# Splitting the operands of two LayerNorm sums into two float32r parts

## The chip, the cores and the metric

The kernel runs on one core of one Trainium2 chip. The metric is the device time of one launch in microseconds (us), as the median of several runs. The profile is of one execution; its times are given from the start of its span.

## The reference

The reference is one decoder layer on 1024 tokens of 1024 channels. An input projection feeds two branches: stick-breaking attention with 8 heads, and a convolution branch. Both are gated, merged, projected once more, and normalised with the residual. The change lies in the convolution branch:

```python
c = glu_a * jax.nn.sigmoid(glu_b)
c = causal_depthwise_conv(c, conv_w, conv_b)                    # 512 channels, 31 taps
c = jax.nn.silu(layer_norm(c, conv_ln_g, conv_ln_b))            # over the 512 channels
conv_branch = jnp.einsum('bsc,cd->bsd', c * jax.nn.silu(z_conv), w_conv_proj) + b_conv_proj
```

`layer_norm` subtracts the mean over the channels, divides by the root of the variance plus 1e-5, and applies a gain and an offset.

## The kernel before

Everything stands with channels on the 128 partitions and the 1024 tokens along the free dimension, so the convolution's 512 channels are four tiles `cacc[0]` to `cacc[3]` of 128x1024. Almost every matmul works on float32 data that was split into two float32r parts, a high part (`wh`, `xh`, `tah`, ...) rounded by a copy, and a low part (`wl`, `xl`, `tal`, ...) that is the difference. `mm_piece` (L204 to 217) multiplies one piece of weights, 128x512, into one PSUM bank with three products: high by high, high by low and low by high, twelve matmuls of 512 columns in all.

The instruction order of every engine is fixed when the program is built. A planner, the class `Timeline`, keeps a clock for TensorE (`tl.t`) and for the other engines, with a cost for each operation, and writes an instruction into its engine's queue when its turn comes in that model. Side tasks are generators: one yields an operation for ScalarE ("A"), VectorE ("V") or GpSimd ("G") and goes on when the planner thinks it done. Among operations that are ready for one engine, the planner takes the lowest urgency number first (0 for what frees a PSUM bank, 1 and 2 for most others), and among equals the one that became ready first. On the chip each engine then works through its queue in that order.

`conv_norm` (L610) is the LayerNorm over channels. It adds the four `cacc` tiles on VectorE into `lnsum`. `total` (L617) multiplies the 1024 columns of `lnsum` by a 128x128 matrix of 1/512 (`ones`), as two float32 matmuls of 512 columns, which puts the mean of every token on all partitions of the banks `mps`. Eight subtractions (urgency 0) take the mean from `cacc`. Squares, their sum `lnq` and `variances` follow; a small chain on 128x8 values gives the reciprocal root. Eight instructions spread it onto diagonals (`lndg`, 128x1024), and a second `total` turns it into rows `rps` that all partitions hold. `finish(i)` (L670) multiplies `cacc[i]` by `rps`, takes a sigmoid on ScalarE, applies gain and offset, and multiplies by the sigmoid; two tiles are in work at a time. Before each `total`, `yield tl.now + LAG` holds the matmuls back by 3 us of the planner's clock, so that TensorE, which runs in order, does not stand waiting for them.

This runs beside the stage `run_pairs` (L1022). There pairs of weight blocks, numbered 0 to 11, are multiplied in a scheme with five products per pair here, P5, P6, P7, P4, P3, each one piece of `mm_piece` into a bank `sps`. The pairs follow one another, but the last two are interleaved: P5 and P6 of pair 10, P5 and P6 of pair 11, and then the rest (L863). `make_s(n)` (L899) loads the two blocks of a pair (`rc`, 512 KB each) and forms its operands on VectorE. One buffer `s` serves three of them in turn, so that each step waits until the split of the one before is done: S1 for P5 (`s<-rc`), S2 for P6 (`s<-s,rc`), S4 for P3 (`s<-rc,s`).

```python
        while "S1" not in done:
            yield tl.now + 100
        yield vtt(1, s, s, ra[:, lo_], ALU.subtract)
        have["S2"] = s
```

`split_operand` (L929) makes `wh` on ScalarE and `wl` on VectorE (urgency 1) for each piece. `feed` (L268) lets at most five pieces be split and not yet used up (`N_SPL`). At most two pairs are in work (`N_PAIR`): the loads of pair 11 are issued when the planner sees all five splits of pair 9 done, and S1 of pair 11 is queued when the planner sees the loads landed. Results of the pairs leave PSUM by VectorE (`u`, `c`, urgency 0) in `pair_out`. `split_att` (`attb`, `ach`, `acl`) prepares the attention branch for the matmuls that follow the pairs (`dps<-ach`); it is begun for one of its four tiles at P5 of pairs 8, 9, 10 and 11. The products of the convolution branch start only after the pairs and after `make_cc`, which needs `finish` of all four tiles.

VectorE and ScalarE operations that are issued through helpers show in the profile under the helper's line: L406 (`act`), L409 (`vtt`), L412 (`vstt`). So they are told apart by tile names.

Of the kernel before, what the change touches and what calls it, by code (L numbers as in the profile page):

```python
# [10 lines left out]
F32R = mybir.dt.float32r  # L11
AF = mybir.ActivationFunctionType
ALU = mybir.AluOpType

P = 128
S = 1024
# [7 lines left out]
HALF = 512  # L24
# [150 lines left out]
def layer_kernel(ctx: ExitStack, tc, xT, x, wv, wd, wa, wc, wo, vec, bv, lng, lnb, cst, out):  # L175
    nc = tc.nc
# [7 lines left out]
    tl = Timeline()  # L184
    live = {"ps": 0, "hf": 0}

    def blk(name, dt=F32):
        return blkp.tile([P, S], dt, name=name, tag="blk")
# [5 lines left out]
    def bank(name):  # L194
        live["ps"] += 1
        return psp.tile([P, HALF], F32, name=name, tag="ps")

    def drop(kind, n=1):
        live[kind] -= n

    def f32(ap):
        return ap.bitcast(F32)

    def pe_ns(n):  # L204
        return n / 2.4 + 13.3
# [25 lines left out]
    ones = const.tile([P, P], F32, name="ones")  # L231
    nc.vector.memset(ones, 1.0 / (NC * P))
    ones_r = const.tile([P, P], F32R, name="ones_r")
# [4 lines left out]
    def vcol(i, rows=slice(0, P)):  # L238
        return vecs[rows, i:i + 1]
# [165 lines left out]
    def act(u, out, in_, func=AF.Copy, n=HALF, **kw):  # L405
        return "A", u, n, (lambda: nc.scalar.activation(out, in_, func, **kw)), (BIAS if "bias" in kw else {})  # L406

    def vtt(u, out, a, b, op, n=HALF):
        return "V", u, n, lambda: nc.vector.tensor_tensor(out, a, b, op=op)  # L409

    def vstt(u, out, a, s, b, op0, op1, n=HALF, ptr=True):
        return "V", u, n, (lambda: nc.vector.scalar_tensor_tensor(out, a, s, b, op0, op1)), (PTR if ptr else {})  # L412
# [126 lines left out]
    def start_cc():  # L539
        if flags["conv"] and flags["pairs"]:  # L540
            for i in range(NC):
                tl.spawn(make_cc(i), tl.now)
# [28 lines left out]
    def conv_block(i):  # L571
# [21 lines left out]
        def last():  # L593
            yield vtt(9, b[:, ev], b[:, ev], a[:, ev], ALU.subtract)
            yield vtt(9, a[:, 1:HALF], a[:, 1:HALF], a[:, HALF:S - 1], ALU.add, HALF)
            yield vtt(9, a[:, od], b[:, ev], a[:, od], ALU.subtract)
            yield "V", 9, S, lambda: nc.vector.tensor_scalar(a, a, vcol(CONVB + i), None, op0=ALU.add), {"per": 0.521}
            conv_stat["on"] -= 1
            conv_stat["done"] += 1
            start_conv()  # L600
            if conv_stat["done"] == NC:
                tl.spawn(conv_norm(), tl.t)
# [7 lines left out]
    def conv_norm():  # L610
        hs = [slice(0, HALF), slice(HALF, S)]
        s = blk("lnsum")
        yield vtt(1, s, cacc[0], cacc[1], ALU.add, S)
        for i in (2, 3):
            yield vtt(1, s, s, cacc[i], ALU.add, S)

        def total(src, name):  # L617
            r = [bank(name) for _ in hs]
            for ps, c in zip(r, hs):
                nc.tensor.matmul(ps, ones, src[:, c], start=True, stop=True)  # L620
                tl.t += 4 * pe_ns(HALF)
            return r

        got = []
        yield tl.now + LAG
        yield lambda: got.extend(total(s, "mps"))
        mps = list(got)
        yield [vtt(0, cacc[i][:, c], cacc[i][:, c], ps, ALU.subtract) for i in range(NC) for ps, c in zip(mps, hs)]
        drop("ps", 2)
        q = None  # L630
        for i in range(NC):
            qi = blk(f"lnq{i}")
            yield act(0, qi, cacc[i], AF.Square, n=S)
            if i:
                yield vtt(1, q, q, qi, ALU.add, S)
            else:
                q = qi


        def variances():  # L640
            ps = bank("vps")
            for b in range(NT):
                nc.tensor.matmul(ps[:, b:b + 1], q[:, b * P:(b + 1) * P], ones[:, 0:1], start=b == 0, stop=b == NT - 1)
                tl.t += 4 * 109
            return ps

        got.clear()
        yield tl.now + LAG
        yield lambda: got.append(variances())
        vps = got[0]  # L650
        lt = blk("lnt")
        sd, r, t2 = (lt[:, k * NT:(k + 1) * NT] for k in range(3))
        yield "A", 0, NT, lambda: nc.scalar.activation(sd, vps[:, 0:NT], AF.Sqrt, bias=epsc[:, 0:1]), {"extra": 1300}
        yield "V", 1, NT, lambda: nc.vector.reciprocal(r, sd), {"per": 6.2}
        yield vtt(1, t2, r, r, ALU.mult, NT)
        yield vstt(1, t2, vps[:, 0:NT], epsc[:, 0:1], t2, ALU.add, ALU.mult, NT)
        drop("ps")
        yield "V", 1, NT, lambda: nc.vector.tensor_scalar(t2, t2, -0.5, 1.5, op0=ALU.mult, op1=ALU.add), {"per": 0.521}

        yield vstt(1, r, r, float(NC * P), t2, ALU.mult, ALU.mult, NT, ptr=False)  # L660
        dg = blk("lndg")
        yield [("V", 1, P, (lambda b=b: nc.vector.tensor_scalar(dg[:, b * P:(b + 1) * P], ident, r[:, b:b + 1], None,
                                                               op0=ALU.mult)), {"per": 0.521}) for b in range(NT)]
        got.clear()
        yield tl.now + LAG
        yield lambda: got.extend(total(dg, "rps"))
        rps = list(got)
        left, left_r = [NC], [NC]

        def finish(i):  # L670
            a, g = cacc[i], blk(f"lng{i}")
            yield [vtt(1, a[:, c], a[:, c], ps, ALU.mult) for ps, c in zip(rps, hs)]
            left_r[0] -= 1
            if left_r[0] == 0:
                drop("ps", 2)
            yield act(0, g, a, AF.Sigmoid, n=S, bias=vcol(LNB + i), scale=vcol(LNG + i))
            yield "V", 1, S, lambda: nc.vector.tensor_scalar(a, a, vcol(LNG + i), vcol(LNB + i), op0=ALU.mult,
                                                             op1=ALU.add), {"per": 0.521}
            yield vtt(1, a, a, g, ALU.mult, S)
            left[0] -= 1  # L680
            if left[0] == 0:
                flags["conv"] = True
                start_cc()
            elif i + 2 < NC:
                tl.spawn(finish(i + 2), tl.now)

        for i in range(2):
            tl.spawn(finish(i), tl.now)
# [420 lines left out]
    for k in range(NK):  # L1109
# [9 lines left out]
        for c0 in range(0, S, step):  # L1119
            c = slice(c0, c0 + step)  # L1120
# [133 lines left out]
    def cuts(tb):  # L1254
        return [0, HALF, HALF + 256, D] if tb == NT - 1 else [0, HALF, D]
# [43 lines left out]
    for d in range(NK):  # L1299
        while not {2 * d, 2 * d + 1} <= wo_there:  # L1300
            tl.skip()
        for tb in range(first):
            for n in range(2):
                tt, c = slice(tb * P, (tb + 1) * P), slice(n * HALF, (n + 1) * HALF)
# [9 lines left out]
    for tb in range(first, NT):  # L1314
        load_row(tb)
        tt = slice(tb * P, (tb + 1) * P)
        for n in range(len(cuts(tb)) - 1):
            c = slice(cuts(tb)[n], cuts(tb)[n + 1])
# [3 lines left out]
            ps = bank("yps")[:, 0:w]  # L1322
# [30 lines left out]
    c = slice(0, N_TAIL)  # L1353
# [56 lines left out]
```

## Time and the profile before

| | |
|---|---|
| median of 3 runs | 760.25 us (759.88 to 760.5) |
| profiled execution, its own time | 760.05 us |
| its span | 758.2 us |
| mean granted TensorE clock | 0.997 |
| TensorE busy (matmul) | 743.2 us, 98% |
| VectorE busy | 624.1 us, 82% |
| ScalarE busy | 348.4 us, 46% |

The time is the span plus 1.85 us around it. Busy shares are means over stages with different limits. In the lists an instruction is shown by engine, line, operation and `out<-in` tiles; a matmul's duration is longer than the step from one to the next, since they are pipelined.

### The profile page before, as it was taken

To read this page: it belongs to the slowest core of one execution; us is meant where nothing else is said; L and a number is where in the kernel's file an instruction comes from. 1 tells how busy PE (TensorE), PEld (TensorE's weight loads), DVE (VectorE), ACT (ScalarE), POOL (GpSimd) and SP (SyncE) were. 2 spreads that over 40 slices of the span, in tenths; PEclk is the share of its full clock that TensorE was granted. 3 is DMA by queue.
4 is the path that set the end of the run, shared out by engine and by line. 5 is a ranking of instruction groups with operands and counts; after the bars stand their busy time and mean duration, and the time that the engine had idled before them with its cause. 6 is when DMAs were issued, how large, how long until landed. Compare 5 with 4: busy or idle time off the path is not lost.

```text
span 758.2 us, 10189 instructions
## 1 busy us (share of the span) xinstructions
PE 743.2 (98%) x3630; PEld 622.8 (82%) x3630; DVE 624.1 (82%) x950; ACT 348.4 (46%) x652; POOL 117.5 (15%) x128
## 2 busy tenths in 40 slices
PE   9999999999999999999999999999999999999995
PEld 7888888889888888888888888787878888888885
DVE  7537779999998639999999999999996759920985
ACT  2119757279677745876443433355542323410100
POOL 3312330413432332040200000000000033000000
PEclk9999999999999999999999999999999999999998
DMA  7553543544754448286653453355547865530052
GB/s 229 181 189 114 98 91 63 98 97 78 170 110 103 85 71 192 56 246 207 176 200 131 155 178 123 132 190 168 207 153 239 282 228 198 198 117 1 0 202 75
DMA packets 51972, 110.60 MB, mean 146 GB/s; under 512 B 6225, under 2 KB 11217, under 8 KB 51922
## 3 DMA queue, kind: packets, MB, share of 16 engines
q1 hardware_dynamic: 41474, 96.26, 37.5%
q0 software_dynamic: 10304, 13.64, 12.4%
q8 instruction: 28, 0.46, 0.2%
q14 instruction: 22, 0.18, 0.1%
q10 hardware_dynamic: 144, 0.07, 0.0%
HBM read 81.62 MB, written 24.12 MB: 139 GB/s over the span
## 4 chain that ended last, share of the span: by engine, by line
PE 79%; DVE 17%; issue 1%; ACT 1%; DMA 1%; POOL 0%; SPq 0%; DVEq 0%; ACTq 0%; POOLq 0%
PE dps L216 11%; PE dps L211 10%; PE dps L212 10%; PE sps L211 7%; PE sps L212 7%; PE sps L216 7%; PE vps L1130 6%; DVE cacc L412 5%; PE pvps L777 4%; PE yps L222 4%; PE yps L223 4%; PE yps L224 4%; PE tps L754 4%; DVE f L739 3%; DVE cs L412 2%; PE zps L727 1%
## 5 line engine op out<-in xcount | busy, mean ns | idle before, releaser
L211 PE MATMUL dps<-xh,wh 128*128 128x512 f32 x352 | 141.1, 401 | 0.0
L212 PE MATMUL dps<-xl,wh 128*128 128x512 f32 x352 | 137.6, 391 | 0.0
L216 PE MATMUL dps<-xh,wl 128*128 128x512 f32 x352 | 99.3, 396 | 0.0
L739 DVE TENSOR_TENSOR_SCAN f<-f,eyez 128x896 f32<-128x896 f32 (+3 forms) x64 | 83.2, 1341 | 5.8 <-ACT f L406 5.8
L412 DVE SCALAR_TENSOR_TENSOR cacc<-cin,vecs,cacc 128x511 f32<-128x511 f32 (+14 forms) x116 | 82.7, 739 | 0.0
L252 POOL TENSOR_TENSOR wl<-wr,wh 128x512 fp32r<-128x512 f32 x22 | 30.9, 1410 | 302.5 <-ACT wh L248 302.5
L212 PEld LDWEIGHTS dps<-xl,wh 128*128 128x128 f32 x352 | 66.3, 188 | 12.3
L211 PEld LDWEIGHTS dps<-xh,wh 128*128 128x128 f32 x352 | 66.2, 188 | 12.3
L216 PEld LDWEIGHTS dps<-xh,wl 128*128 128x128 f32 x352 | 64.0, 188 | 11.9
L248 ACT ACTIVATE wh<-wr 128x512 fp32r<-128x512 f32 x80 | 50.5, 636 | 46.6 <-DMA wr<-wv 26.6
L796 POOL DMA_DIRECT2D att<-pvt x64 | 56.5, 991 | 95.1 <-ACT pvt L406 61.3
L406 ACT ACTIVATE wth<-tps 128x384 fp32r<-128x384 f32 (+1 forms) x80 | 43.7, 567 | 45.0 <-PE tps L754 44.4
L409 DVE TENSOR_TENSOR wtl<-tps,wth 128x384 fp32r<-128x384 f32 (+1 forms) x80 | 48.9, 628 | 18.7 <-ACT wth L406 17.7
L255 POOL DMA_DIRECT2D wl<-wd x36 | 32.9, 915 | 125.2 <-ACT wl L254 89.5
L223 PE MATMUL yps<-wol,mh 128*128 128x512 f32 (+1 forms) x136 | 51.2, 377 | 0.0
L224 PE MATMUL yps<-woh,ml 128*128 128x512 f32 (+1 forms) x136 | 51.2, 376 | 0.0
L222 PE MATMUL yps<-woh,mh 128*128 128x512 f32 (+1 forms) x136 | 51.2, 376 | 0.0
L754 PE MATMUL tps<-eyez,f 128*128 128x128 f32 x288 | 42.9, 275 | 2.6 <-DVE f L739 2.6
L412 DVE SCALAR_TENSOR_TENSOR cs<-cs,hs__77 128x511 f32<-128x511 f32 (+14 forms) x60 | 44.3, 739 | 0.1
L412 DVE SCALAR_TENSOR_TENSOR xrow<-xrow,yps 128x512 f32<-128x512 f32 (+1 forms) x17 | 10.7, 653 | 39.8 <-PE yps L224 39.7
L406 ACT ACTIVATE f<-zps 128x384 f32<-128x384 f32 (+2 forms) x96 | 40.2, 530 | 3.3 <-PE zps L727 3.2
L777 PE MATMUL pvps<-wtl,v 128*128 128x256 f32 (+1 forms) x160 | 40.2, 287 | 0.7 <-DVE wtl L409 0.3
(173 smaller groups left out, 1689.1 us busy)
## 6 DMA issues: line engine op xcount, KB each, us to landing
wr<-wd SPq DMA_DIRECT2D x56, 256.0 KB, 3.0
rc<-wd SPq DMA_DIRECT2D x24, 512.0 KB, 5.7
wl<-wd POOLq DMA_DIRECT2D x36, 256.0 KB, 4.9
c<-c SPq DMA_DIRECT2D x36, 256.0 KB, 2.4
att<-pvt POOLq DMA_DIRECT2D x64, 64.0 KB, 3.4
ga<-c SPq DMA_DIRECT2D x8, 512.0 KB, 6.5
wor<-wo SPq DMA_DIRECT2D x16, 256.0 KB, 6.2
gc<-c SPq DMA_DIRECT2D x8, 512.0 KB, 6.8
```

Source lines behind the costliest of these rows:

```text
L211: nc.tensor.matmul(ps, wh[:, kk], mh, start=first and kk is ks[0], stop=False)
L212: nc.tensor.matmul(ps, wh[:, kk], ml, start=False, stop=False)
L216: nc.tensor.matmul(ps, wl[:, kk], mh, start=False, stop=last and kk is ks[3])
L222: nc.tensor.matmul(ps, wh, mh, start=first, stop=False)
L223: nc.tensor.matmul(ps, wh, ml, start=False, stop=False)
L224: nc.tensor.matmul(ps, wl, mh, start=False, stop=last)
L406: return "A", u, n, (lambda: nc.scalar.activation(out, in_, func, **kw)), (BIAS if "bias" in kw else {})
L412: return "V", u, n, (lambda: nc.vector.scalar_tensor_tensor(out, a, s, b, op0, op1)), (PTR if ptr else {})
L739: u.ready[tb] = yield ("V", 2, n, lambda: nc.vector.tensor_tensor_scan(f[:, 0:n][:, ::-1], f[:, 0:n][:, ::-1], eyez[:, S - n:S][:, ::-1], ...
L754: nc.tensor.transpose(ps[:, o:o + P], u.f[tb][:, j * P:(j + 1) * P], ident)
L777: nc.tensor.matmul(u.ps[:, 0:n], st, wt[:, jj * 256:jj * 256 + n], start=(i == m and jj == 0 and wt is wh), stop=(i == 0 and jj == 1 and w ...
L796: e = yield "G", 1, 0, (lambda part=part: nc.gpsimd.dma_start(dst, tmp[part, 0:256], accum_op=ALU.add)), {"extra": 430}
```

## The change

Before each of the two sums, a new generator `parted` makes two float32r tiles of the 128x1024 operand: a copy on ScalarE (high part) and a subtraction on VectorE (low part). `total` then multiplies each 512-column half of both parts by `ones_r`, a float32r copy of the same matrix that the kernel already holds, and adds them in PSUM. The planner's charge for one half falls from four matmul steps to two. Two more blocks are taken from the pool of 128x1024 tiles for each sum. `variances` keeps float32.

```diff
             for ps, c in zip(r, hs):
-                nc.tensor.matmul(ps, ones, src[:, c], start=True, stop=True)
-                tl.t += 4 * pe_ns(HALF)
+                for part in src:
+                    nc.tensor.matmul(ps, ones_r, part[:, c], start=part is src[0], stop=part is src[1])
+                tl.t += 2 * pe_ns(HALF)
             return r
 
+        def parted(src, name, got):
+
+            h, l = blk(f"{name}h", F32R), blk(f"{name}l", F32R)
+            yield act(1, h, src, n=S)
+            yield vtt(1, l, src, f32(h), ALU.subtract, S)
+            got.extend((h, l))
+
         got = []
+        sp = []
+        yield from parted(s, "lnsum", sp)
         yield tl.now + LAG
-        yield lambda: got.extend(total(s, "mps"))
+        yield lambda: got.extend(total(sp, "mps"))
...
         got.clear()
+        dp = []
+        yield from parted(dg, "lndg", dp)
         yield tl.now + LAG
-        yield lambda: got.extend(total(dg, "rps"))
+        yield lambda: got.extend(total(dp, "rps"))
```

## Rows read from the trace of the kernel before

**Rows 1.** Page, part 1: busy us (share of the span) and instructions of two engines.

```profile
PE 743.2 (98%) x3630; PEld 622.8 (82%) x3630; DVE 624.1 (82%) x950; ACT 348.4 (46%) x652; POOL 117.5 (15%) x128
```

**Rows 2.** Busy time by stretch, us: length, PE, PEld, DVE, ACT, POOL, granted clock, DMA share.

```profile
474.00:486.00 12.00, 12.00 (x51) 9.24 (x50) 11.93 (x18) 3.52 (x7) 0.00 (x0) 1.00 0.45 155
486.00:502.00 16.00, 16.00 (x72) 13.26 (x71) 15.96 (x25) 9.02 (x13) 0.00 (x0) 1.00 0.41 132
502.00:520.00 18.00, 18.00 (x85) 14.45 (x84) 16.98 (x38) 9.82 (x14) 0.00 (x0) 1.00 0.48 159
520.00:540.00 20.00, 20.00 (x90) 16.57 (x89) 20.00 (x31) 10.62 (x15) 0.00 (x0) 1.00 0.65 217
540.00:560.00 20.00, 18.12 (x78) 14.09 (x77) 19.20 (x32) 8.94 (x15) 0.00 (x0) 1.00 0.64 232
560.00:577.00 17.00, 17.00 (x76) 14.08 (x76) 16.64 (x28) 8.28 (x14) 0.00 (x0) 1.00 0.31 103
```

**Rows 3.** Waits of PE from 370 to 758 us: total us, times, longest.

```profile
PE sps L211 <- ACT wh L406: 1.9, 2, 1.3
```

**Rows 4.** Timeline of PE, 550 to 557 us: start, duration, [idle before <- releaser].

```profile
552.63 0.50 PE L211 MATMUL sps<-tah,wh 128*128 128x512 f32 x1 [1.28 <-ACT wh L406]
...
556.24 0.50 PE L211 MATMUL sps<-tah,wh 128*128 128x512 f32 x1 [0.60 <-ACT wh L406]
```

**Rows 5.** Timeline of DVE: operand steps and splits of pair 9, S1 of pair 11.

```profile
523.48 0.68 DVE L409 TENSOR_TENSOR wl<-s,wh 128x512 fp32r<-128x512 f32 x1
...
527.61 0.68 DVE L409 TENSOR_TENSOR s<-s,rc 128x512 f32<-128x512 f32 x1
...
537.99 0.69 DVE L409 TENSOR_TENSOR s<-rc,s 128x512 f32<-128x512 f32 x1
...
543.93 0.68 DVE L409 TENSOR_TENSOR wl<-s,wh 128x512 fp32r<-128x512 f32 x1
...
551.14 0.69 DVE L409 TENSOR_TENSOR s<-rc 128x512 f32<-128x512 f32 x1
```

**Rows 6.** Timeline of DVE: where the LayerNorm's steps stand.

```profile
478.77 1.22 DVE L409 TENSOR_TENSOR lnsum<-lnsum,cacc 128x1024 f32<-128x1024 f32 x1
...
485.56 4.87 DVE L409 TENSOR_TENSOR cacc<-cacc,mps 128x512 f32<-128x512 f32 x8
...
517.31 2.47 DVE L409 TENSOR_TENSOR cacc<-cacc,rps 128x512 f32<-128x512 f32 x4
...
539.80 1.22 DVE L409 TENSOR_TENSOR cacc<-cacc,lng 128x1024 f32<-128x1024 f32 x1
```

**Rows 7.** Chain that ended last, 478 to 519 us: start, share of the chain, what.

```profile
480.93 1.72 PE mps L620 x4
...
513.10 0.91 PE sps L216 x4
...
514.46 1.72 PE rps L620 x4
```

**Rows 8.** Groups of instructions: count, busy us, mean ns of one.

```profile
L409 DVE TENSOR_TENSOR tbl<-tb,tbh 128x1024 fp32r<-128x1024 f32 x4 | 4.9, 1218 | 0.0
...
L406 ACT ACTIVATE tah<-ta 128x1024 fp32r<-128x1024 f32 x4 | 4.2, 1056 | 0.0
```

**Rows 9.** Timeline of DVE: a 1024-wide operation and the next one's start.

```profile
534.33 1.22 DVE L409 TENSOR_TENSOR cacc<-cacc,lng 128x1024 f32<-128x1024 f32 x1
535.46 0.69 DVE L409 TENSOR_TENSOR wl<-rc,wh 128x512 fp32r<-128x512 f32 x1
```

**Rows 10.** Timeline of DVE and PE: last split of the attention operands, first and later matmuls on them.

```profile
572.45 0.69 DVE L409 TENSOR_TENSOR acl<-attb,ach 128x512 fp32r<-128x512 f32 x1
575.46 0.39 PE L211 MATMUL dps<-ach,wh 128*128 128x512 f32 x1
...
579.76 0.39 PE L212 MATMUL dps<-acl,wh 128*128 128x512 f32 x1
```

## The prediction

> **What bounds the kernel now.** I read the page's busy shares first, then busy time by stretch around the LayerNorm, then what TensorE waited for, then the timelines of TensorE and VectorE there. TensorE is busy 98% of the span [rows 1], so what shortens its work can show in full, as long as nothing else takes the time back. By stretches [rows 2] the reader is to see two things. TensorE has no gap from 474 to 540 us, and again from 560 on, but it lacks 1.88 us between 540 and 560. And VectorE, whose share over the whole span is only 82%, is here as full as TensorE: 11.93 + 15.96 + 16.98 + 20.00 + 19.20 = 84.07 us of the 86 us from 474 to 560. The LayerNorm runs in just this stage. The waits of TensorE say that from 370 us to the end it stood still only twice, 1.9 us together, both times for a `wh` of ScalarE [rows 3]; its timeline puts them at 552.63 (1.28 us) and 556.24 (0.60 us) [rows 4]. From 474 to 577 us the stage has two bounds close together, TensorE's own work and VectorE's queue.
>
> **Why TensorE stood still there.** Going back from 552.63: that matmul is P5 of pair 11, and its `wh` is a copy of S1 of pair 11, which VectorE made at 551.14 [rows 5]. That step's place in VectorE's queue was given by the planner: the loads of pair 11 come after the last split of pair 9. Followed in the queue, pair 9 goes: split of S1 at 523.48, S2 at 527.61, S4 at 537.99, split of S4 at 543.93, done 544.6 [rows 5]. From there to 551.14 are 6.5 us, which the planner reserves for the loads of 1 MB. So each wait in VectorE's queue on the way from 523 to 544 us pushes P5 of pair 11 out. What filled that queue was `finish`: its first multiplication by `rps` stands at 517.31, its last product at 539.80 [rows 6], over the same 20 us.
>
> **The change, part by part.**
>
> *Matmuls.* In the chain the four instructions of a float32 `total` (two per half) hold TensorE 1.72 us, and four float32r matmuls of 512 columns hold it 0.91 us [rows 7]. After the change a `total` is four float32r matmuls. Each saves 1.72 - 0.91 = 0.81 us, both 1.62 us. That those four run at the pace of the neighbours is what I take; they have the same form, 128x128 weights with 512 float32r columns. The bounds are 0 (they run as slow as float32) and 1.62.
>
> *ScalarE.* Two more copies of 128x1024 at 1.06 us [rows 8], 2.1 us together. ScalarE is busy 3.52 of 12 us from 474 and 9.82 of 18 us from 502 [rows 2], so its idle time covers them. Without that cover the price would be a `wh` later by up to 1.06 us, which the splits made ahead take up.
>
> *VectorE.* Two more subtractions of 128x1024, like `tbl<-tb,tbh` at 1218 ns [rows 8]. They are pipelined: after a 1024-wide one that began at 534.33 the next began at 535.46 [rows 9], so each takes 1.13 us of the queue, 2.26 us together. Nothing hides these by itself: VectorE has 86 - 84.07 = 1.93 us free before 560 [rows 2]. Behind them in the queue stand the splits `wl`, the operands `s`, and the PSUM reads. The bounds of what they cost TensorE are 0, if its stock of splits covers them, and 2.26 us, if all of it arrives at 556.24.
>
> *Order.* The chain of the LayerNorm grows twice by a copy (1.06 us) and a subtraction (1.13 us) ahead of the 3 us of LAG, plus a turn behind one or two 0.6 us operations, less the 0.81 us that `total` takes less: by about 2 us each time. With the first subtraction's own 1.13 us in the queue, `finish` begins some 4 to 5 us later, at about 522 instead of 517.31. This is not a cost by itself: the convolution's products come after the pairs, behind 577 us, and `finish` was over at 541 [rows 6]. But it moves 12 us of VectorE work (8 at 0.60, 4 at 0.72, 4 at 1.13) against the splits of pair 9. At the head of pair 9's chain, before 523, some 4 us of `finish` no longer stand in front of the split of S1 and of S2; these come about 4 us earlier, and the later links (split of S2, S4, split of S4) stay in the crowd as before. Pair 9 is then done at about 541 rather than 544.6, S1 of pair 11 stands at about 547.5 rather than 551.14, and P5 of pair 11 could start at 549. TensorE was ready for it at 552.63 - 1.28 = 551.35 and would be now at 551.35 - 1.62 = 549.7. So the first stop of 1.28 us goes. The second, 0.60 us, lies in the steps S1, split, S2, copy of pair 11 itself; I leave it as it is. The bounds of the stop are 0 and, with all 2.26 us of VectorE and the earlier arrival of TensorE, 1.88 + 1.62 + 2.26 = 5.8 us.
>
> *Blocks.* Four more tiles are taken from the pool of 43. The kernel's tiles alive at this point, counted in the code, are at most about 40, so I cost this at nothing; if one had to wait, it would be a load `rc`, on SP's queue, and pair 11 would be later again.
>
> *Sum.* 760.05 - 1.62 - 1.28 = 757.15 us for the profiled execution; the median shown lies 0.2 us above it, so 757.4 us.
>
> **A rule that speaks against it.** The row shows TensorE stopped behind ScalarE and VectorE, with VectorE full [rows 2, 4]. The Trainium skill, "Perfetto Trace Analysis", section "Optimization Strategies", says that where the matmul engine is idle waiting for others, it is those others that should be relieved. This change loads one of them more. By the rule the sum would be 760.25 + 2.26 = 762.5 us, and the trace bears out its condition, that VectorE has no room; whether its later work or its place in the order decides, the rows of before can't tell. That is the second rival below.
>
> **The rivals.**
>
> *The stop stays, the matmuls save.* The two stops are 1.88 us as before, because the later `finish` falls on the later links of pair 9 and on pair 10 as hard as it fell on the earlier ones. For it: 20.00 of 20 us busy from 520 to 540, wherever one puts things. The time is 760.25 - 1.62 = 758.6 us.
>
> *VectorE's queue sets the end of the stage* (the other side). S1 of pair 11 comes later by up to the 2.26 us that were added, and the matmuls' saving only makes TensorE wait longer at the same place. After 556.24 TensorE has no gap, so the whole time moves by what that matmul moves: 760.25 + 2.26 = 762.5 us. Where half of it is taken up by VectorE's free 1.93 us, it is about 761, within what counts as no change. It decides from the point where pair 9's last split comes later than 543.93. Against it: from 523 to 544 us more than half of the links' time was waiting behind others in the queue, and part of those others leaves.
>
> *The change gives nothing at the matmuls*, since the float32r sums run no faster or the planner moves another task into their place: about 760.25 - 0.3 or so. Against it: the neighbours' 0.91 us [rows 7].
>
> *The attention products become the next stop.* If the pairs end 3.5 us earlier, the first `dps<-ach` come at 572 instead of 575.46. The last `acl` ended at 573.1, and its matmul ran at 579.76 [rows 10]: 6.6 us of room, less 3.5, less 2.26 of later VectorE. That leaves 0.8 us, so nothing is lost; if the order is worse there, some 1 to 2 us.
>
> **How the numbers follow.** A run's median here tells differences of about 0.2%, or 1.5 us. Both stops shrink or the first goes (757.4; with both gone 756.75): 0.42. The stop stays (758.6, just past the bound): 0.18. The stop grows by about what the matmuls save, or they save nothing (759 to 761.7): 0.23. VectorE sets the end (about 762.5): 0.12. Something else, such as a late load or the attention operands, to either side: 0.05. Faster by over 0.2%: 0.42, two thirds to three quarters of 0.18, and a little of the last, 0.57. Slower by over 0.2%: 0.12 and some of the neighbouring cases, 0.16. Within: 0.27. The range goes from 756.5, both stops gone, to 761.7, where a good part of VectorE's 2.26 us comes through; the full 762.5 is left out.
>
> **What would show it.** In the changed kernel's profile: `mps` and `rps` with four matmuls each, 0.91 us in the chain instead of 1.72; two subtractions and two copies of 128x1024 more; the first `cacc<-cacc,rps` near 522; S1 of pair 11 at 549 or earlier; and TensorE's wait for `wh` near 0.6 us. The prediction is wrong if that wait is 3 us or more, if TensorE waits at a new place between 480 and 580 us (for a `wl`, for `acl`, or at the sums themselves for the low part, should VectorE run behind the planner's clock by more than the 3 us of LAG), or if the gap-free stretch after 580 us is broken.

## The result, and the profile after

The changed kernel took 764.64 us (763.93 to 766.72, 4 runs) beside 760.38 us for the kernel before on the same chip; the ratio is 1.0057, 95% interval 1.0045 to 1.0069. So it became slower by about 4.3 us, where 2.9 us less was forecast, and the time lies outside the range. Single runs of one kernel scatter by 1 to 3 us, because the first part of the program, which is the same in all, ends later in some: in the fourteen profiled executions TensorE either began 11 to 13 matmuls from 6 to 9 us, and the first addition of `lnsum` stood at 475.3 to 475.9 us, or it began 7, and the addition stood at 476.8 to 478.3. Where two traces are set side by side below, times are therefore also counted from that addition, which stands at 475.30 us in the profiled execution before and at 477.09 in the one after.

The waits of TensorE from 370 us to the end, which answer to [rows 3]:

```profile
PE sps L216 <- DVE wl L409: 2.6, 2, 2.3
PE sps L211 <- ACT wh L406: 2.1, 1, 2.1
```

They were 1.9 us, all for a `wh`; now they are 4.8 us, and more than half is for a `wl` of VectorE. The timeline of TensorE shows the places, beside [rows 4]; the last rows show its pace:

```profile
550.67 1.19 PE L216 MATMUL sps<-tah,wl 128*128 128x512 f32 x4 [0.37 <-DVE wl L409]
...
555.94 2.01 PE L216 MATMUL sps<-tah,wl 128*128 128x512 f32 x4 [2.26 <-DVE wl L409]
560.10 0.79 PE L211 MATMUL sps<-tah,wh 128*128 128x512 f32 x1 [2.15 <-ACT wh L406]
...
561.12 0.63 PE L211 MATMUL sps<-tah,wh 128*128 128x512 f32 x1
561.54 0.63 PE L212 MATMUL sps<-tal,wh 128*128 128x512 f32 x1
...
568.56 0.39 PE L211 MATMUL sps<-tbh,wh 128*128 128x512 f32 x1
...
569.01 0.39 PE L211 MATMUL sps<-tbh,wh 128*128 128x512 f32 x1
569.24 0.39 PE L212 MATMUL sps<-tbl,wh 128*128 128x512 f32 x1
```

The first of the three waits, 0.37 us, is for the `wl` of P6 of pair 10. P5 of pair 11 now gets its `wh` in time, but stands for its `wl`; P6 of pair 11 stands for its `wh`. And there is a second loss that is no wait: from 556 to 566 us matmuls of 512 columns follow one another every 0.43 us instead of every 0.23. Busy time by stretch names it (length, PE, PEld, DVE, ACT, POOL, granted clock, DMA share):

```profile
550.00:554.00 4.00, 3.31 (x14) 2.17 (x12) 4.00 (x7) 0.00 (x0) 0.00 (x0) 1.00 0.98 365
554.00:558.00 4.00, 2.01 (x4) 1.09 (x4) 4.00 (x7) 0.80 (x2) 0.00 (x0) 0.76 0.60 210
558.00:562.00 4.00, 1.90 (x5) 1.52 (x6) 4.00 (x8) 2.02 (x4) 0.00 (x0) 0.50 0.01 4
562.00:566.00 4.00, 4.00 (x11) 3.12 (x10) 2.78 (x5) 1.82 (x3) 0.00 (x0) 0.50 0.00 0
566.00:570.00 4.00, 4.00 (x19) 3.25 (x18) 3.35 (x7) 0.63 (x1) 0.00 (x0) 0.96 0.00 0
```

The granted clock is 0.50 from 558 to 566, that is 1.2 instead of 2.4 GHz. The trace has its fall at 556.0 us, just behind the stop of 2.26 us, so that the four matmuls from 555.94, 2.01 us long, are already slow; it is back at 1.00 from 566.3, with TensorE at work without a gap since 560.10. In the kernel before it stayed at 1.00 through both its stops [rows 2]. The Trainium skill, "TensorE: Matmul & The Clock Gate", section "Part 1: The HAM clock gate (the "warmup" mystery)", says that the lower clock is the default and activity releases it; the trace agrees, with the fall behind a stop and the rise in a gapless stretch.

VectorE's timeline, from the first product by `rps` to the stops, beside [rows 5] and [rows 6]:

```profile
524.94 1.88 DVE L409 TENSOR_TENSOR cacc<-cacc,rps 128x512 f32<-128x512 f32 x3
...
541.29 0.68 DVE L409 TENSOR_TENSOR cacc<-cacc,rps 128x512 f32<-128x512 f32 x1
...
548.01 0.68 DVE L409 TENSOR_TENSOR s<-rc 128x512 f32<-128x512 f32 x1
...
550.54 1.21 DVE L409 TENSOR_TENSOR cacc<-cacc,lng 128x1024 f32<-128x1024 f32 x1
...
553.48 1.21 DVE L409 TENSOR_TENSOR cacc<-cacc,lng 128x1024 f32<-128x1024 f32 x1
...
555.21 0.68 DVE L409 TENSOR_TENSOR wl<-s,wh 128x512 fp32r<-128x512 f32 x1
...
558.22 0.68 DVE L409 TENSOR_TENSOR s<-s,rc 128x512 f32<-128x512 f32 x1
```

S1 of pair 11 (`s<-rc`) did come early: 70.92 us after the first addition of `lnsum`, where it had been 75.84. Its `wh` was done at 549.5 on ScalarE. But its `wl` stands at 555.21, behind the last steps of `finish` for the third and fourth tile, and S2 (558.22), which needs that split done, after it. In the kernel before, `finish` was over at 541 [rows 6].

The sums themselves did what was said; the chain for the first one, beside [rows 7] (the four matmuls of `rps` follow one another every 0.23 us too):

```profile
485.44 0.91 PE mps L621 x4
```

**Where the 6.67 us between the two profiled executions are** (766.72 and 760.05). The first addition of `lnsum` is 1.79 us later; that is the scatter of the start. From there to P6 of pair 11 it takes 83.01 us instead of 80.94: 2.07 more. That is 1.62 less for the sums, 2.90 more of waiting (0.37 + 2.26 + 2.15 - 1.88), and 0.80 for the four matmuls between the stops at the low clock (1.71 instead of 0.91). From P6 of pair 11 to the second piece after it takes 8.46 us (560.10 to 568.56) instead of 5.62 (556.24 to 561.86): 2.84 for the clock. Together 6.70. Without the start, some 4.9 us belong to the change in these two executions, within the 3.4 to 5.2 of the interval. The line of the kernel before at which that second piece begins:

```profile
561.86 0.39 PE L211 MATMUL sps<-tbh,wh 128*128 128x512 f32 x1
```

### The profile page after: what moved, and what is told of

Its sections match the earlier page's. It is cut to its first block, busy times and chain, and to the rows that moved or that the text cites. A ratio compares the mean times of both kernels' runs of the same rounds, so it can differ in the third digit from the quotient of the medians.

```text
span 765.0 us, 10206 instructions
## 1 busy us (share of the span) xinstructions
PE 746.9 (98%) x3630; PEld 626.7 (82%) x3630; DVE 626.5 (82%) x952; ACT 350.9 (46%) x654; POOL 116.3 (15%) x128
## 4 chain that ended last, share of the span: by engine, by line
PE 77%; DVE 19%; issue 2%; ACT 1%; DMA 1%; POOL 0%; SPq 0%; DVEq 0%; ACTq 0%; POOLq 0%
PE dps L216 11%; PE dps L211 10%; PE dps L212 10%; PE sps L211 6%; PE sps L212 6%; PE sps L216 6%; PE vps L1142 6%; DVE cacc L412 5%; PE pvps L789 4%; PE yps L224 4%; PE yps L223 4%; PE yps L222 4%; PE tps L766 4%; DVE f L751 3%; DVE cs L412 2%
```

## The experiments

All are compared with the kernel before on the same chip. The columns of the table: the ratio with its interval; P6 of pair 11, counted from the first addition of `lnsum`; the stops of TensorE at pairs 10 and 11; VectorE's work and idle time from that addition to S2 of pair 11; and the first `yps` matmul, counted from that addition too, which holds everything the change can do and not the scatter of the start. All but the ratio are from the profiled execution, so they are of one execution each. From the first `yps` to the end every kernel here takes the same 95.7 to 95.8 us.

| kernel | ratio (interval) | P6 of pair 11 | stops | work + idle | first yps |
|---|---|---|---|---|---|
| before | 1 | 80.94 | 1.88 | 78.33 + 1.13 | 187.2 |
| changed | 1.0057 (1.0045 to 1.0069) | 83.01 | 4.78 | 80.06 + 1.07 | 192.1 |
| matmuls alone | 1.0009 (1.0001 to 1.0018) | 81.14 | 3.71 | 78.83 + 0.82 | 187.4 |
| operands alone | 1.0076 (1.0064 to 1.0088) | 85.14 | 4.38 | 80.28 + 3.35 | 191.8 |
| delay alone | 1.0074 (1.0061 to 1.0087) | 83.66 | 4.52 | 78.13 + 3.66 | 191.5 |
| work alone | 1.0073 (1.0061 to 1.0086) | 85.08 | 5.88 | 80.77 + 2.42 | 193.2 |
| low parts on GpSimd | 1.0082 (1.0068 to 1.0096) | 85.23 | 7.50 | 81.36 + 2.39 | 193.9 |
| first sum only | 1.0017 (1.0007 to 1.0027) | 80.96 | 3.16 | 78.44 + 1.01 | 188.8 |
| second sum only | 1.0049 (1.0034 to 1.0063) | 82.96 | 4.64 | 80.54 + 0.89 | 192.0 |
| shorter LAG | 1.0061 (1.0045 to 1.0077) | 83.24 | 5.61 | 80.33 + 1.00 | 190.8 |
| stops filled | 1.0022 (1.0011 to 1.0033) | 83.03 | 1.46 | 80.07 + 1.07 | 189.3 |
| before, finish last | 0.9967 (0.9954 to 0.9979) | 78.41 | 0 | 68.67 + 1.17 | 184.5 |
| changed, finish last | 0.9958 (0.9945 to 0.9970) | 76.68 | 0 | 72.27 + 1.07 | 182.8 |
| changed, late half last | 0.9941 (0.9926 to 0.9956) | 76.69 | 0 | 72.76 + 1.07 | 182.8 |

### The matmuls alone

Against the kernel before, the lines that matter (`lndg` becomes float32r like `lnsumr`, and the planner's charge is that of the change):

```diff
-        for i in (2, 3):
-            yield vtt(1, s, s, cacc[i], ALU.add, S)
+        sr = blk("lnsumr", F32R)
+        yield vtt(1, s, s, cacc[2], ALU.add, S)
+        yield vtt(1, sr, s, cacc[3], ALU.add, S)
...
-                nc.tensor.matmul(ps, ones, src[:, c], start=True, stop=True)
...
+                for n in range(2):
+                    nc.tensor.matmul(ps, ones_r, src[:, c], start=n == 0, stop=n == 1)
...
-        yield lambda: got.extend(total(s, "mps"))
+        yield lambda: got.extend(total(sr, "mps"))
...
-        dg = blk("lndg")
+        dg = blk("lndg", F32R)
```

> The float32r matmuls of the change without its copies and subtractions: lnsum's last addition and the diagonals are written as float32r at once, and each half adds that one part twice (so the low part is left out and the sum is doubled). Theory A (the time went into where finish now falls against the splits of pairs 10 and 11, because the chain grew by a copy and a subtraction): finish stays about where it was or begins up to 1 us earlier, the stops stay near 1.9 us, TensorE's clock stays at full speed in the pairs, and the time is 1 to 2 us below before. Rival (any shift of the order costs 3 us and more): 762 or more.

It came out about level with before, not 1 to 2 us faster. `finish` began where it was, but its last product moved from 64.5 to 68.2 us after the first addition, and the stops grew by 1.83 us, about what the sums saved (1.62). P6 of pair 11 stood where it was, within 0.2 us: TensorE only came to wait earlier. So VectorE's queue sets that point, and cheaper matmuls ahead of it gain nothing. The expectation missed this. The granted clock stayed at 1.00 in this execution, though its first stop was 2.67 us long.

### The operands alone

Against the kernel before; `parted` is that of the change, and `total` keeps its float32 matmuls:

```diff
+        sp = []
+        yield from parted(s, "lnsum", sp)
         yield tl.now + LAG
         yield lambda: got.extend(total(s, "mps"))
...
+        dp = []
+        yield from parted(dg, "lndg", dp)
         yield tl.now + LAG
         yield lambda: got.extend(total(dg, "rps"))
```

> The change's copies and subtractions with the old float32 matmuls (the parts are made and not used). Theory A: finish begins some 6 us later as in the change, TensorE's stops in the pairs are 4 us or more, the clock falls to half speed after them, and the time is 4 to 7 us above before, 1.6 us more than the change at most. Rival B (the float32r matmuls themselves or the planner's shorter charge for them cause it): within 1 us of before or at most 2.3 us above it.

5.8 us above before by the ratio, as the first theory said. Its `finish` moved further than that theory had it: the first product by `rps` comes 10.2 us later than in the kernel before, not some 6. The loss comes with the operands; the float32r matmuls are not its cause.

### The delay alone

```diff
-        yield tl.now + LAG
+        yield tl.now + LAG + 2200
         yield lambda: got.extend(total(s, "mps"))
...
-        yield tl.now + LAG
+        yield tl.now + LAG + 3700
         yield lambda: got.extend(total(dg, "rps"))
```

> The kernel before with the two float32 sums held back by 2.2 and 3.7 us more of the planner's clock, and nothing added to any engine. Theory A (the place of finish decides, not the 2.26 us of VectorE work): the stops grow to 3 us or more and the time is 2 to 6 us above before. Rival C (the added work on VectorE decides): within 1 us of before.

5.6 us slower with no work added to any engine. Busy time by stretch, beside the third of [rows 2]:

```profile
502.00:520.00 18.00, 18.00 (x89) 15.18 (x88) 15.07 (x33) 9.69 (x15) 0.00 (x0) 1.00 0.47 160
```

VectorE, which had 16.98 us of work in these 18 us, has 15.07. The work that it could not yet do lies behind, in front of the splits of pairs 10 and 11: 3.66 us idle ahead of S2 of pair 11 instead of 1.13, and P6 of pair 11 comes 2.72 us later. So added work on VectorE is not needed to be slow, and neither are the copies on ScalarE or the four tiles from the pool, which this kernel does not have.

### The work alone

```diff
+        def extra(src, name):
+            yield vtt(1, blk(name), src, cacc[0], ALU.subtract, S)
...
+        tl.spawn(extra(s, "ex0"), tl.now)
         yield tl.now + LAG
...
+        tl.spawn(extra(dg, "ex1"), tl.now)
         yield tl.now + LAG
```

> The kernel before with two more 128x1024 subtractions on VectorE at the places of the two low parts, that nobody waits for, and no other change. Rival C (the added 2.26 us on VectorE decides): the stops grow by about 2 us and the time is 2 us or more above before. Theory A (the place of finish decides): the price is smaller than that of the delay alone (5 us), 0 to 2.5 us.

5.5 us slower. Nobody waits for these two subtractions, and yet the whole price is there; the expectation that the work alone costs less than the delay alone fell. The reason is in the table: the 2.26 us of work went ahead of S2 of pair 11 in full (2.44 more), and since the LayerNorm's own steps stand behind it in the queue, these moved too (the last product of `finish` to 554.3), with 1.29 us more of idle time. So work and delay are not two theories; here either puts the late half of `finish` on the splits of pairs 10 and 11.

### The low parts on GpSimd

```diff
-            yield vtt(1, l, src, f32(h), ALU.subtract, S)
+            yield "G", 1, S, lambda: nc.gpsimd.tensor_tensor(l, src, f32(h), op=ALU.subtract)
```

> The changed kernel with the two low parts made on GpSimd, which is idle in this stage, instead of VectorE: VectorE has its old amount of work, and the chain grows by more than in the change. Theory A (the place of finish decides): stops of 3 us or more and a time of 2 to 6 us above before. Rival C (VectorE's added work decides): the stops are back at about 1.9 us and the time is 1 to 2 us below before.

6.2 us slower, though VectorE has its old amount of work in all: the later chain put 3.0 us more of it ahead of S2 of pair 11 (81.36 against 78.33). So taking the work off the full engine is not enough while the chain grows.

### One sum of the two

```diff
-        yield from parted(dg, "lndg", dp)
...
-        yield lambda: got.extend(total(dp, "rps"))
+        yield lambda: got.extend(total32(dg, "rps"))
```

`total32` is the old `total`.

> The change for the mean's sum alone; the second sum keeps float32. Counted from the first addition of lnsum, P6 of pair 11 began 80.94 us later in the kernel before and 83.01 in the changed one. Theory Q (VectorE works without a gap and in order, and all of finish stands ahead of pair 11's S2, so that each us of work or of idle time put ahead of it arrives there): 82.0 to 82.5, and the time is 1 to 1.5 us above before, or up to 4 if the stop is long enough for the clock to fall. Theory A (the place of finish alone): finish moves by half as much, the stops are between, 80 to 83, without a rule.

> The change for the second sum (the reciprocal roots) alone; the mean's sum keeps float32. Theory Q: P6 of pair 11 at 82.0 to 82.5 us after the first addition of lnsum, the time 1 to 1.5 us above before, up to 4 with the clock. Theory A: as for e9, between 80 and 83.

The second is the same edit on `lnsum`, with the change left for `lndg`. Each adds 1.13 us of VectorE work. The first left P6 of pair 11 where it was (80.96) and cost 1.3 us by the ratio, with one stop of 3.16 us and a clock of 0.87 from 560 to 570; since P6 of pair 11 did not move and the first `yps` came 1.6 us later, its whole loss lies behind that stop, in the slow matmuls. The second moved it by 2.02 us, nearly as far as both together. So the rule that each microsecond put ahead arrives, which had both at 82.0 to 82.5, does not hold: in the one case the planner put as much other work behind S2 as came in front (78.44 against 78.33), in the other it put 2.2 us ahead for 1.13 added.

### A shorter LAG

```diff
-        yield tl.now + LAG
+        yield tl.now + LAG - 1500
         yield lambda: got.extend(total(sp, "mps"))
...
-        yield tl.now + LAG
+        yield tl.now + LAG - 2500
         yield lambda: got.extend(total(dp, "rps"))
```

> The changed kernel with the waits ahead of the two sums cut by 1.5 and 2.5 us, which brings finish back to within some 2 us of its old place; the added work stays. Theory A (the place of finish): P6 of pair 11 near 81.3 us after the first addition of lnsum, the clock at full speed, and the time within 1 us of before. Theory Q: the work ahead is the same, so P6 of pair 11 stays at 82.5 to 83.2, and the time is 1 to 4.5 us above before.

As slow as the change. It tells less than it was meant to: the first product by `rps` came back by 1.8 us, but the last of `finish` by only 0.4, so the late half stayed on the same splits.

### The stops filled

In `mm_piece`, with `fill[0]` at 1 for P5 of pair 11, at 2 for P6 of pair 11 and at 0 otherwise:

```diff
+        fills = (fill[0] in (1, 2)) * 9
+        if fill[0] == 2:
+            for _ in range(fills):
+                nc.tensor.matmul(ps, zero_r, movs[0][0], start=True, stop=True)
...
+        if fill[0] == 1:
+            for _ in range(fills):
+                nc.tensor.matmul(ps, zero_r, movs[0][0], start=False, stop=False)
         for kk, (mh, ml) in zip(ks, movs):
             nc.tensor.matmul(ps, wl[:, kk], mh, start=False, stop=last and kk is ks[3])
```

> The changed kernel with nine more matmuls of 512 columns on weights of zero in front of the low-part matmuls of P5 of pair 11, and nine in front of P6 of pair 11, into the bank of that piece; they add nothing to the result and the planner doesn't charge them. Theory D (about 3 us of the loss is the clock, which fell to half speed after the stops): the granted clock stays at full speed in the pairs, and the time is 2 to 3.5 us below the change (761 to 762.5). Rival (the slow matmuls after the stops cost nothing, since VectorE sets the pace there): the same time as the change, 764 to 765, or up to 1 us more.

TensorE did eighteen matmuls more and the kernel was faster than the changed one: a ratio of 1.0022 instead of 1.0057, 2.7 us. Its timeline:

```profile
550.69 1.20 PE L225 MATMUL sps<-tah,wl 128*128 128x512 f32 x4 [0.37 <-DVE wl L420]
...
555.97 1.21 PE L225 MATMUL sps<-tah,wl 128*128 128x512 f32 x4 [0.22 <-DVE wl L420]
...
560.13 0.50 PE L217 MATMUL sps<-tah,wh 128*128 128x512 f32 x1 [0.87 <-ACT wh L417]
```

The three ends of waiting are the same as in the changed kernel within 0.03 us, so VectorE sets them. What differs is the clock after them, at 1.00 in stretches that showed 0.50:

```profile
558.00:562.00 4.00, 3.13 (x14) 2.14 (x13) 4.00 (x8) 2.06 (x4) 0.00 (x0) 1.00 0.00 0
562.00:566.00 4.00, 4.00 (x20) 3.31 (x19) 3.90 (x7) 2.31 (x4) 0.00 (x0) 1.00 0.00 0
```

The first `yps` comes 2.8 us earlier than in the changed kernel, the 2.84 us read from the trace above. What is left, 2.1 us over before, is the later end of the stops.

### finish behind the splits

```diff
-            yield [vtt(1, a[:, c], a[:, c], ps, ALU.mult) for ps, c in zip(rps, hs)]
+            yield [vtt(2, a[:, c], a[:, c], ps, ALU.mult) for ps, c in zip(rps, hs)]
...
-            yield "V", 1, S, lambda: nc.vector.tensor_scalar(a, a, vcol(LNG + i), ...)
-            yield vtt(1, a, a, g, ALU.mult, S)
+            yield "V", 2, S, lambda: nc.vector.tensor_scalar(a, a, vcol(LNG + i), ...)
+            yield vtt(2, a, a, g, ALU.mult, S)
```

This was done on the changed kernel, on the kernel before, and on the changed kernel for the third and fourth tile alone (`u = 1 if i < 2 else 2`).

> The changed kernel with the VectorE steps of finish at urgency 2 instead of 1, so that the splits and operands of the pairs go before them. Theory A: the stops at pairs 10 and 11 shrink to under 1 us, the clock stays at full speed, and the time is 1.5 to 3.5 us below before (757 to 759). Rival C (VectorE has too little room for 2.26 us more, whatever the order): 761 or more.

> The kernel before with the VectorE steps of finish at urgency 2, as in e4_after_finish_last. Theory A: with the splits first there is no stop at pairs 10 and 11 or hardly one, so the time is 1 to 1.9 us below before (758.4 to 759.3), and e4, which has the two cheaper sums besides, lies 1.3 to 1.8 us below this one. Rival (the gain of e4 comes all from the order, the float32r sums being worth nothing): as fast as e4, 757.

> The changed kernel with the VectorE steps of finish at urgency 2 for the third and fourth tile alone, those that fell on the splits of pairs 10 and 11. They are 4 at 0.60, 2 at 0.72 and 2 at 1.13 us, 6.1 us, more than the two stops of 4.4 us that can be read at P5 and P6 of pair 11. Theories Q and A: no stop or under 0.5 us, the clock at full speed, the time within 0.7 us of e4_after_finish_last (757.0). Rival (it takes both halves, or the gain of e4 came from elsewhere): 759 or more.

All three were faster than before, at medians of 757.01, 758.72 and 756.96 us. By the ratios the kernel before gained 2.5 us, more than its 1.88 us of stops and than the 1 to 1.9 expected; what the rest is stays open. TensorE has no stop left; the stretch of the last one, beside the fifth of [rows 2]:

```profile
550.00:560.00 10.00, 10.00 (x46) 8.29 (x45) 10.00 (x18) 4.16 (x7) 0.00 (x0) 1.00 0.47 181
```

VectorE is as full as ever (10.00 of 10 us), and still has the added work. On the changed kernel the last product of `finish` now begins at 580 to 584 us, on the kernel before at 559, and TensorE waits for nothing behind it. Moving the eight steps of the late half is enough: with them behind the splits S2 of pair 11 stands 73.83 us after the first addition instead of 81.13. Between the first two, both without a stop, the first `yps` differs by 1.7 us (184.5 and 182.8): here the 1.62 us of the cheaper sums arrive. By the ratios the two differ by less, 0.7 us, with intervals that overlap, so the size of that gain is not settled.

## Why the prediction was wrong, point by point

*What bounds the stage.* Right: VectorE is as full as TensorE there, and its queue sets the stops at P5 and P6 of pair 11. The matmuls alone showed it most plainly.

*The matmuls.* Right: 0.91 us instead of 1.72 in the chain, and in the two profiled executions with `finish` last 1.7 us at the end, once nothing gives it back.

*ScalarE at nothing.* Its copies took their 1.06 us each and stood in no wait of TensorE; no run tested them by themselves, but the delay alone and the work alone lost as much without them.

*Blocks at nothing.* S1 of pair 11, which waits for the loads, stood 4.9 us earlier, so no load came late there.

*The shift of `finish` and pair 9.* Right in direction and about in size: 47.8 us from the first addition to the first product by `rps` instead of 42.0, which is 5.8 later where 4 to 5 was said, and S1 of pair 11 earlier by 4.9 us where 3.6 was said. The wait for the `wh` of P5 of pair 11 went as forecast.

*The step that failed* is the one behind it: "So the first stop of 1.28 us goes. The second, 0.60 us, lies in the steps S1, split, S2, copy of pair 11 itself; I leave it as it is." The working followed `finish` away from pair 9 and not to where it went. That late half, 4 at 0.60, 2 at 0.72 and 2 at 1.13 us, stood from 541 to 555, in front of the split of P5 of pair 11, and S2 waits for that split. So the stops became 4.78 us, where 0.60 was forecast; the prediction's own sign of being wrong, a wait for a `wl`, is the longest of them. The term for VectorE's work was set at 0 for that reason too; its upper bound, 2.26 us, is about what P6 of pair 11 moved, 2.07. But that this equals the added work is not a rule: the delay alone, without any, gave 2.72, and the first sum alone, with 1.13, gave 0.02.

*The term that was missing* is the clock. The prediction had no price for a TensorE that works again after a stop; the trace of before showed none, since the clock held through its stops of 1.28 and 0.60 us. It was 2.84 us, the larger half of the loss in the profiled execution; filling the stops gave back 2.7 us by the ratios.

*The rivals.* "VectorE's queue sets the end of the stage" came nearest, at 762.5 us without the clock; with its 2.84 us it would have been 765.3, beside 764.64 measured. It was right that VectorE's queue moves P6 of pair 11 and that the matmuls' saving goes into waiting. But it had this come through a later S1 of pair 11 and a later end of pair 9; S1 came 4.9 us earlier, and what came later was its split and S2 (81.13 against 79.46). That the 2.26 us come near is luck, as the delay alone and the first sum alone show. The case "the stop stays" named half of the mechanism, `finish` on later links, but on those of pairs 9 and 10, and priced it at no growth. The attention products were never a stop in any run.

What stays open is why the planner's order turns 1.13 us of work into nothing in one place and into 2 us in another; the table shows how much came to stand ahead, and not a rule for it.

## What to carry to other kernels

When work moves in an in-order queue that is full, ask what it will stand in front of at its new place, and not only what it stops hindering; work that nobody needs soon belongs behind the splits that the bound engine waits for, and here that one urgency number was worth more (2.5 us on the kernel before) than the cheaper matmuls (1.62 us). A saving on an engine that then waits at the next stop gains nothing until the stop is gone. And a stop of TensorE may cost twice: the wait, and the matmuls at the low clock after it.

## What the runs showed of the hardware

Behind a stop of 2.26 us the granted clock of the changed kernel fell to 0.50, and it stayed there for 10.2 us, over a second stop of 2.15 us; matmuls of 512 columns then followed one another every 0.43 us instead of every 0.23. With eighteen matmuls on weights of zero in these stops the clock stayed at 1.00. The length of a stop does not settle it: one of 3.16 us (the first sum only) brought the clock down from 559.1 to 562.5 us, one of 2.67 us with 0.76 and 0.28 behind it (the matmuls alone) left it at 1.00. A float32 matmul of 512 columns took 0.86 us (two instructions of 0.43), and a float32r one 0.23, so that two float32r parts cost about half of one float32 sum.
